# Expert activation in two column halves, transposes copied by two engines, gate products first for 128 slots

## The chip, the cores and the metric

The kernel runs on one core of a Trainium2 chip. The metric is the device time of one execution in microseconds (us). The core's engines work side by side, each on its own queue in order: TensorE (PE; its weight loads are listed as PEld), VectorE (DVE), ScalarE (ACT), GpSimd (POOL) and SyncE (SP), which here issues DMAs. Semaphores order them against each other. Matmul results land in PSUM, which has eight banks of 512 float32 columns on 128 partitions.

## The reference

One transformer block on 512 tokens of width 1024: a normalised, modulated input, a gated MLP and a gated delta network side by side, and then 32 experts, of which each token uses four. The change touches the experts alone:

```python
def expert_block(args):
    tok, wt, e = args
    xb = h_pad[tok]
    gu = xb @ w_gu[e] + b_gu[e]
    gate = jnp.minimum(gu[:, :D_FF], SWIGLU_LIMIT)
    up = jnp.clip(gu[:, D_FF:], -SWIGLU_LIMIT, SWIGLU_LIMIT)
    act = gate * jax.nn.sigmoid(SWIGLU_ALPHA * gate) * (up + 1)
    return (act @ w_down[e] + b_down[e]) * wt[:, None]
```

The width of gate, up and the output is 1024, the limit 7, alpha 1.702, all in float32.

## The kernel before

The first part (up to about 400 us) computes the block ahead of the experts and the routing. Then `run(p, ...)` is called for 32 experts one after the other. An expert's weights are 12 chunks of 1 MB: eight of gate and up (128 rows of 2048 columns), four of down. They pass through a ring of 14 buffers that SyncE fills in order; a buffer is filled again when the matmuls of its last chunk are done.

Experts are sorted by their number of tokens and each gets a fixed number of slots: 14 get 64, three get 32, seven get 96, four get 128, three get 160 and one 192. 128 slots are a `Wide` unit; the others are `Unit`s of 64 or 32 slots (96 is 64 + 32, 160 is 128 + 32, 192 is 128 + 64). The slots of a `Unit` of n stand on n partitions, and the columns are laid out in 128/n blocks over the partitions, so that its gate and up are tiles of 128 partitions by w = 1024 n/128 columns: 512 columns for 64 slots (gate and up in a bank each), 256 for 32 slots (gate and up in one bank).

`run` issues for each expert, in this order: the gate/up matmuls chunk by chunk (`gu_chunk`, or `gu_parts` for `Wide`, which does all gate columns of a chunk before its up columns); `act` of each unit; `between`, which gives TensorE the transposes of the next expert's rows (line 1306) and, for some, the search of the one after that; `down_start` (a small bias matmul), ahead of `turn` or behind it; `turn`, which transposes the activated tile on TensorE (line 1462; for `Wide` 1528) and copies the transposes from one PSUM bank to SBUF (line 1464; for `Wide` 1530, and 1531 for a residual); then the down matmuls chunk by chunk. A down matmul of chunk f takes one transposed block of 128 columns of the activation as its stationary operand. All engines run in the order of the code (a manual schedule), and a tile layer sets the semaphores.

`act` calls `swiglu`, five operations on one tile: Relu (line 1402) and Sigmoid (1403) on ScalarE give sigmoid(1.702 min(gate, 7)); VectorE clips up (1404), makes the gate product min(gate, 7) times that sigmoid (1405), and the product with up + 1 (1406). `gu` in the profile is a PSUM tile (gate, up, or the transposes), `f` the activation's tiles in SBUF, `at` and `ath` the copied transposes.

Of the kernel before, what the change touches and what calls it, by code (L numbers as in the profile page):

```python
# [11 lines left out]
AF = mybir.ActivationFunctionType  # L12
OP = mybir.AluOpType
# [43 lines left out]
def hybrid_block(tc, x, c, w_ada, b_ada, norm1_w, w_in, gm_vnorm_w, gm_w_spatial, gm_b_spatial,  # L57
# [3 lines left out]
    V, S, G, T = nc.vector, nc.scalar, nc.gpsimd, nc.tensor  # L61
# [236 lines left out]
    for n in range(5):  # L298
        V.tensor_scalar(ta[:, 0, :], ta[:, 2, :], n, 1, op0=OP.logical_shift_right,
                        op1=OP.bitwise_or)  # L300
# [459 lines left out]
    def turn(gs):  # L760
        V.transpose(xd[:, gs, :].rearrange("p c i -> p (c i)"), xtd[:, gs, :].rearrange("p c i -> p (c i)"))

    halves = [slice(0, 8), slice(8, 16)]
    for gs in halves:
        turn(gs)
    fill()
    for n in range(4):
        p1s = []
        for gs in halves:
            p1 = bank([P, 8, 32])  # L770
            p1s.append(p1)
            for c8 in range(8):
                for q in range(4):
                    r = slice(q * 32, q * 32 + 32)
                    mm(p1[r, c8, :], ms[n][r, gs.start + c8, :], xd[r, gs.start + c8, :])
        for gs, p1 in zip(halves, p1s):
            S.activation(w1[:, gs, :], p1, AF.Copy)
        fill()
        p2s = []
        for gs in halves:  # L780
            p2 = bank([P, 8, 32])
            p2s.append(p2)
            for c8 in range(8):
                for q in range(4):
                    r = slice(q * 32, q * 32 + 32)
                    mm(p2[r, c8, :], w1[r, gs.start + c8, :], xtd[r, gs.start + c8, :])
        for gs, p2 in zip(halves, p2s):
            V.tensor_tensor(xtd[:, gs, :], xtd[:, gs, :], p2, op=OP.subtract)
            turn(gs)
        fill()  # L790
# [32 lines left out]
    for g in range(4):  # L823
        gs = slice(g * 4, g * 4 + 4)
        kk = bank([P, 4, 2, CH])
        for c4 in range(4):
            ch, hp = divmod(g * 4 + c4, 2)
            for hb in range(2):
                r = slice(hb * 64, hb * 64 + 64)
# [23 lines left out]
    for g in range(2):  # L853
        for hb in range(2):
            r = slice(hb * 64, hb * 64 + 64)
# [318 lines left out]
    both = range(2)  # L1174
# [62 lines left out]
    act_tiles = [f16[:, 2 + i // 2, (i % 2) * 512:(i % 2) * 512 + 512] for i in range(4)]  # L1237
# [158 lines left out]

        return ((h[0], w[0]), (h[1], w[0]), (h[0], w[1]))

    def swiglu(gate, up, r, u):

        n = gate.shape[0]
        S.activation(r, gate, AF.Relu, scale=-1.0, bias=sevens[0:n, 0:1])  # L1402
        S.activation(r, r, AF.Sigmoid, scale=-1.702, bias=sevens[0:n, 1:2])  # L1403
        V.tensor_scalar(u, up, 7.0, -7.0, op0=OP.min, op1=OP.max)  # L1404
        V.scalar_tensor_tensor(r, gate, 7.0, r, op0=OP.min, op1=OP.mult)  # L1405
        V.scalar_tensor_tensor(u, u, 1.0, r, op0=OP.add, op1=OP.mult)  # L1406
        return u

    class Unit:

# [42 lines left out]
        def act(self):  # L1453
            i = (0, 1) if not self.second else (0, 2) if self.part.first else (2, 3)
            r, u = (act_tiles[j][:, 0:self.w] for j in i)
            self.a = swiglu(self.gate, self.up, r, u)

        def turn(self):
            nj = self.w // P
            t = psG.tile([P, 4, P], F32, name="gu")[:, 0:nj]  # L1460
            for j in range(nj):
                T.transpose(t[:, j, :], self.a[:, j * P:(j + 1) * P], ident)  # L1462
            self.at = mp.tile([P, 4, P], F32, name="at", tag="hx" if self.second else "ath", bufs=1)[:, 0:nj]
            S.activation(self.at, t, AF.Copy)  # L1464

        def down_mm(self, l, src, start, stop):
            n, w = self.n, self.w
# [29 lines left out]
    class Wide:  # L1497
# [20 lines left out]
                    mm(self.gu[c * 2 + q], l[:, k, :], r[:, q * 512:q * 512 + 512], False, k == KC - 1 and i == 2)  # L1518

        def act(self):  # L1520
            self.a = [swiglu(self.gu[c], self.gu[2 + c], act_tiles[2 * c], act_tiles[2 * c + 1]) for c in both]

        def turn(self):
            self.at, self.al = (mp.tile([P, KC, P], F32R, name=nm, bufs=1) for nm in ("ath", "atl"))
# [410 lines left out]
```

## Time and profile before

| | us |
|---|---|
| median of three runs | 1533.23 |
| lowest and highest run | 1532.83, 1536.65 |
| the profiled execution | 1535.69 |
| its span, first to last instruction | 1533.9 |
| TensorE busy | 1396.8 (91%) |
| VectorE busy | 698.0 (46%) |
| ScalarE busy | 474.9 (31%) |

Read the busy shares with the stages in mind: the first 400 us are another program than the experts, and a matmul that is listed as busy is not always at its peak. Mean granted TensorE clock: 0.955.

### The profile page before, as it was taken

What the parts mean: (1) busy time and instruction counts of PE and PEld (TensorE: products, weight loads), DVE (VectorE), ACT (ScalarE), POOL (GpSimd) and SP (SyncE); (2) the same over time, 40 slices, a digit from 0 to 9 for tenths busy, and PEclk for the clock granted to TensorE, in tenths of its full rate; (3) what the DMA queues carried; (4) which work ended last, traced back from release to release, by engine and by line L of the source; (5) the groups of instructions that cost most, each with busy time, mean ns of one, the idle gap of its engine ahead of it and who ended that gap; (6) DMA issues with size and microseconds to landing.
All of it is one profiled execution on the core that took longest, in us unless ns stands there. A gap on an engine that the chain in (4) does not pass through costs nothing. (4 is left out here: it accounts for less than half of the span.)

```text
span 1533.9 us, 23341 instructions
## 1 busy us (share of the span) xinstructions
PE 1396.8 (91%) x9113; PEld 729.9 (48%) x9113; DVE 698.0 (46%) x1345; ACT 474.9 (31%) x735; POOL 236.7 (15%) x219
## 2 busy tenths in 40 slices
PE   4898998896899999999999999999999999999982
PEld 3555897674336454337334533642353235424621
DVE  3674639884218454128115612831463136214713
ACT  4343332321116342126014501621351135113501
POOL 2233434340011000110101011000101010101010
PEclk9998999997999999999999999999999999999995
DMA  9566331159699995999999699999988997899972
GB/s 328 181 235 207 98 117 47 52 192 351 245 396 409 401 411 198 400 399 404 390 408 410 253 362 409 407 390 410 398 326 317 403 378 270 314 409 385 382 300 113
DMA packets 113809, 479.54 MB, mean 313 GB/s; under 512 B 15238, under 2 KB 28715, under 8 KB 80922
## 3 DMA queue, kind: packets, MB, share of 16 engines
q1 hardware_dynamic: 98176, 454.10, 75.8%
q0 software_dynamic: 10208, 19.06, 5.0%
q10 hardware_dynamic: 5306, 4.80, 1.0%
q8 instruction: 74, 1.21, 0.3%
q14 instruction: 45, 0.37, 0.1%
HBM read 466.60 MB, written 17.96 MB: 316 GB/s over the span
## 5 line engine op out<-in xcount | busy, mean ns | idle before, releaser
L71 PE MATMUL gu<-ring,h 128*64 128x512 f32 (+1 forms) x1984 | 381.1, 599 | 0.0
L1390 DVE TENSOR_TENSOR wlo<-ring,whi 128x1024 fp32r<-128x1024 f32 x192 | 229.2, 1222 | 49.8 <-ACT whi L1389 48.8
L71 PE MATMUL gu<-ring,at 128*32 128x256 f32 (+1 forms) x1536 | 236.5, 507 | 13.8 <-ACT at L1464 13.8
L1389 ACT ACTIVATE whi<-ring 128x1024 fp32r<-128x1024 f32 x192 | 200.5, 1061 | 113.8 <-PE gu L71 92.0
L71 PEld LDWEIGHTS gu<-ring,h 128*64 128x64 f32 (+1 forms) x1984 | 104.9, 128 | 244.9 <-issue 237.0
L1402 ACT ACTIVATE f<-gu,sevens 128x512 f32<-128x512 f32 (+1 forms) x51 | 32.1, 629 | 533.1 <-PE gu L71 530.9
L1404 DVE TENSOR_SCALAR f<-gu 128x512 f32<-128x512 f32 (+1 forms) x51 | 31.6, 620 | 298.7 <-PE gu L71 281.1
L71 PEld LDWEIGHTS gu<-ring,at 128*32 128x32 f32 (+1 forms) x1536 | 64.2, 125 | 164.8 <-issue 128.6
L1281 POOL DMA_INDIRECT f<-xnd,idx x36 | 36.4, 1012 | 545.3 <-PE gu L1462 280.5
L1750 POOL DMA_INDIRECT acc<-yo,idx x31 | 55.8, 1802 | 401.4 <-DVE yo L1484 237.9
L158 POOL TENSOR_TENSOR wlo<-w,whi 128x1024 fp32r<-128x1024 f32 x32 | 79.3, 2484 | 142.6 <-ACT whi L157 123.1
L71 PE MATMUL gu<-whi,hh 128*128 128x512 f32 x256 | 84.5, 411 | 0.0
L71 PE MATMUL gu<-wlo,hh 128*128 128x512 f32 x256 | 81.1, 398 | 0.8 <-DVE wlo L1390 0.4
L71 PE MATMUL gu<-whi,hl 128*128 128x512 f32 x256 | 80.3, 394 | 0.0
L1484 DVE SCALAR_TENSOR_TENSOR yo<-gu,info,g2x 128x512 f32<-128x512 f32 (+1 forms) x23 | 16.5, 716 | 132.4 <-PE gu L71 132.4
L71 PEld LDWEIGHTS gu<-whi,hh 128*128 128x128 f32 x256 | 45.6, 188 | 33.3 <-ACT whi L1389 18.7
L71 PEld LDWEIGHTS gu<-wlo,hh 128*128 128x128 f32 x256 | 47.6, 188 | 14.2 <-DVE wlo L1390 3.2
L71 PEld LDWEIGHTS gu<-whi,hl 128*128 128x128 f32 x256 | 48.1, 188 | 11.6
L71 PE MATMUL bank<-hhi,whi 128*128 128x512 f32 x160 | 51.5, 442 | 1.8 <-ACT hhi L247 1.8
L71 PE MATMUL gu<-whi,ath 128*128 128x512 f32 x128 | 48.9, 466 | 0.0
L157 ACT ACTIVATE whi<-w 128x1024 fp32r<-128x1024 f32 x32 | 33.7, 1054 | 48.5 <-PE bank L71 26.4
L1462 PE MATMUL gu<-ident,f 128*128 128x128 f32 x114 | 20.1, 301 | 31.4 <-DVE f L1406 31.0
(434 smaller groups left out, 1761.7 us busy)
## 6 DMA issues: line engine op xcount, KB each, us to landing
ring<-in_w_gu_dram SPq DMA_DIRECT2D x256, 1024.0 KB, 16.7
ring<-in_w_down_dram SPq DMA_DIRECT2D x128, 1024.0 KB, 17.8
adaw<-in_w_ada_dram SPq DMA_DIRECT2D x32, 512.0 KB, 4.9
w<-in_w_in_dram SPq DMA_DIRECT2D x24, 512.0 KB, 4.8
ada<-in_w_ada_dram SPq DMA_DIRECT2D x16, 512.0 KB, 10.2
w<-in_w_out_dram SPq DMA_DIRECT2D x8, 512.0 KB, 3.3
x<-in_x_dram SPq DMA_DIRECT2D x4, 512.0 KB, 5.0
x<-in_x_dram ACTq DMA_DIRECT2D x4, 512.0 KB, 4.2
```

The costliest lines, as they stand in the source:

```text
L71: T.matmul(o, l, r, start=start, stop=stop, skip_group_check=True)
L157: S.activation(hi, w, AF.Copy)
L158: G.tensor_tensor(lo, w, hi.bitcast(F32), op=OP.subtract)
L1281: G.indirect_dma_start(out=self.xg, out_offset=None, in_=xnd[:, :], in_offset=bass.IndirectOffsetOnAxis(ap=self.from_[0:self.n], axis=0), ...
L1389: S.activation(hi, w, AF.Copy)
L1390: V.tensor_tensor(lo, w, hi.bitcast(F32), op=OP.subtract)
L1402: S.activation(r, gate, AF.Relu, scale=-1.0, bias=sevens[0:n, 0:1])
L1404: V.tensor_scalar(u, up, 7.0, -7.0, op0=OP.min, op1=OP.max)
L1462: T.transpose(t[:, j, :], self.a[:, j * P:(j + 1) * P], ident)
L1484: V.scalar_tensor_tensor(y, self.dn, self.wt, g2x[self.n], op0=OP.mult, op1=OP.mult)
L1750: G.indirect_dma_start(out=u.rows(acc), out_offset=bass.IndirectOffsetOnAxis(ap=u.idx, axis=0), in_=y, in_offset=None, compute_op=OP.add, ...
```

## The change

`swiglu` is split into four functions, so that its operations can be issued in another order. A `Unit` (32 and 64 slots) now issues the Relu and the Sigmoid for the first half of the columns, then for the second half; on VectorE clip, gate product and product for the first half, then for the second. Its transposes are copied in two halves, the first by ScalarE, the second by VectorE. `Wide` keeps whole tiles of 512 columns, of which it has two: VectorE now does both gate products, then clip and product of the first tile and of the second. The transposes and copies of `Wide` are as before.

```diff
-    def swiglu(gate, up, r, u):
+    def gate_side(gate, r):
 
         n = gate.shape[0]
         S.activation(r, gate, AF.Relu, scale=-1.0, bias=sevens[0:n, 0:1])
         S.activation(r, r, AF.Sigmoid, scale=-1.702, bias=sevens[0:n, 1:2])
+
+    def gate_product(gate, r):
+        V.scalar_tensor_tensor(r, gate, 7.0, r, op0=OP.min, op1=OP.mult)
+
+    def up_side(up, u):
         V.tensor_scalar(u, up, 7.0, -7.0, op0=OP.min, op1=OP.max)
-        V.scalar_tensor_tensor(r, gate, 7.0, r, op0=OP.min, op1=OP.mult)
+
+    def product(r, u):
+
         V.scalar_tensor_tensor(u, u, 1.0, r, op0=OP.add, op1=OP.mult)
-        return u
...
         def act(self):
             i = (0, 1) if not self.second else (0, 2) if self.part.first else (2, 3)
             r, u = (act_tiles[j][:, 0:self.w] for j in i)
-            self.a = swiglu(self.gate, self.up, r, u)
+            self.a = u
+            halves = [slice(0, self.w // 2), slice(self.w // 2, self.w)]
+            for h in halves:
+                gate_side(self.gate[:, h], r[:, h])
+            for h in halves:
+                up_side(self.up[:, h], u[:, h])
+                gate_product(self.gate[:, h], r[:, h])
+                product(r[:, h], u[:, h])
...
-            S.activation(self.at, t, AF.Copy)
+            m = nj // 2
+            S.activation(self.at[:, 0:m], t[:, 0:m], AF.Copy)
+            V.tensor_copy(self.at[:, m:nj], t[:, m:nj])
...
         def act(self):
-            self.a = [swiglu(self.gu[c], self.gu[2 + c], act_tiles[2 * c], act_tiles[2 * c + 1]) for c in both]
+            self.a = [act_tiles[2 * c + 1] for c in both]
+            for c in both:
+                gate_side(self.gu[c], act_tiles[2 * c])
+            for c in both:
+                gate_product(self.gu[c], act_tiles[2 * c])
+            for c in both:
+                up_side(self.gu[2 + c], self.a[c])
+                product(act_tiles[2 * c], self.a[c])
```

In the rows below, which show the built program's order, a name in brackets is the engine whose semaphore is waited for (DMAHW and DMASW are DMA queues).

VectorE's queue in the third expert, which has 64 slots, before (the search's results and indices, then clip, gate product, product; then the next expert's residual):

```order
L1273 COPY info<-t 128x2 [waits PE_49]
L1275 TENSOR_SCALAR idx<-info 64x1 [waits DMASW0_49,DVE_49]
L1425 TENSOR_SCALAR idx<-info,shifts 128x1 [waits DMASW1_49]
L1404 TENSOR_SCALAR f_3753<-gu 128x512 [waits PE_49]
L1405 SCALAR_TENSOR_TENSOR f_3753<-gu,f_3753 128x512 [waits Activation_49]
L1406 SCALAR_TENSOR_TENSOR f_3753<-f_3753 128x512 [waits DVE_49]
L1330 TENSOR_TENSOR hl<-t,hh 128x512 [waits Activation_49]
```

and the same place now:

```order
L1431 TENSOR_SCALAR idx<-info,shifts 128x1 [waits DMASW1_49]
L1409 TENSOR_SCALAR f_3753<-gu 128x256 [waits PE_49]
L1406 SCALAR_TENSOR_TENSOR f_3753<-gu,f_3753 128x256 [waits Activation_49]
L1413 SCALAR_TENSOR_TENSOR f_3753<-f_3753 128x256 [waits DVE_49]
L1409 TENSOR_SCALAR f_3753<-gu 128x256
L1406 SCALAR_TENSOR_TENSOR f_3753<-gu,f_3753 128x256 [waits Activation_49]
L1413 SCALAR_TENSOR_TENSOR f_3753<-f_3753 128x256 [waits DVE_49]
L1479 COPY at<-gu 128x256 [waits Activation_49]
L1330 TENSOR_TENSOR hl<-t,hh 128x512 [waits Activation_49]
```

Three operations have become six of half the width, and VectorE has a copy of the transposes behind them, which waits for ScalarE. The count that the first gate product (1406) waits for is that of the second half's Relu; the count of the copy (1479) is that of ScalarE's copy, whose own count is that of the fourth transpose.

TensorE's queue at the same place, the transposes and the first down matmuls, as a difference:

```order
 L71 MATMUL gu<-b_2219,sel_o 64x512
-L1462 MATMUL gu<-ident,f_3753 128x128 [waits DVE_49]
-L1462 MATMUL gu<-ident,f_3753 128x128 x3
+L1475 MATMUL gu<-ident,f_3753 128x128 [waits DVE_49]
+L1475 MATMUL gu<-ident,f_3753 128x128
+L1475 MATMUL gu<-ident,f_3753 128x128 [waits DVE_49]
+L1475 MATMUL gu<-ident,f_3753 128x128
 L71 MATMUL gu<-ring_3368,at 64x512 [waits DMAHW4_49,Activation_49]
 L71 MATMUL gu<-ring_3368,at 64x512 x3
-L71 MATMUL gu<-ring_3369,at 64x512 [waits DMAHW5_49]
+L71 MATMUL gu<-ring_3369,at 64x512 [waits DMAHW5_49,DVE_49]
```

The transposes now wait twice, once for each half's product; the first down matmul waits for ScalarE's half of the copy, the third chunk's for VectorE's.

VectorE's queue in the fourth expert, with 128 slots, before:

```order
L1390 TENSOR_TENSOR wlo<-ring_3366,whi 128x1024 [waits DMAHW0_49,PE_49,Activation_49]
L1404 TENSOR_SCALAR f_3753<-gu 128x512 [waits PE_49]
L1405 SCALAR_TENSOR_TENSOR f_3753<-gu,f_3753 128x512 [waits Activation_49]
L1406 SCALAR_TENSOR_TENSOR f_3753<-f_3753 128x512 [waits DVE_49]
L1404 TENSOR_SCALAR f_3753<-gu 128x512 [waits PE_49]
L1405 SCALAR_TENSOR_TENSOR f_3753<-gu,f_3753 128x512 [waits Activation_49]
L1406 SCALAR_TENSOR_TENSOR f_3753<-f_3753 128x512 [waits DVE_49]
```

and now:

```order
L1390 TENSOR_TENSOR wlo<-ring_3366,whi 128x1024 [waits DMAHW0_49,PE_49,Activation_49]
L1406 SCALAR_TENSOR_TENSOR f_3753<-gu,f_3753 128x512 [waits Activation_49] x2
L1409 TENSOR_SCALAR f_3753<-gu 128x512 [waits PE_49]
L1413 SCALAR_TENSOR_TENSOR f_3753<-f_3753 128x512 [waits DVE_49]
L1409 TENSOR_SCALAR f_3753<-gu 128x512 [waits PE_49]
L1413 SCALAR_TENSOR_TENSOR f_3753<-f_3753 128x512 [waits DVE_49]
```

Both gate products stand ahead of the first clip, each waiting for its Sigmoid; the first row, the residual of a down chunk, did not move.

## Rows read from the trace of the kernel before

**Rows 1.** Waits: engine, line, releaser, total us, times, longest.

```profile
SPq L1038 <- PE gu L71: 329.9, 173, 11.0
SPq L1041 <- PE gu L71: 219.1, 86, 11.1
...
PEld gu L71 <- DMA ring<-in_w_gu_dram: 8.1, 20, 0.8
```

**Rows 2.** Windows: length, busy us by engine, granted clock, DMA share, GB/s.

```profile
580.00:600.00 20.00, 19.18 (x72) 9.35 (x72) 10.55 (x16) 8.74 (x12) 0.99 (x1) 0.91 0.40 135
714.00:718.00 4.00, 4.00 (x13) 3.11 (x14) 3.15 (x5) 3.43 (x7) 1.01 (x1) 0.57 1.01 420
```

**Rows 3.** Timeline, a 64-slot expert: start, us, engine, line, operation [idle before].

```profile
674.88 0.69 ACT L1402 ACTIVATE f<-gu,sevens 128x512 f32<-128x512 f32 x1 [25.91 <-PE gu L71]
...
675.74 0.69 DVE L1404 TENSOR_SCALAR f<-gu 128x512 f32<-128x512 f32 x1 [10.00 <-PE gu L71]
676.36 0.69 DVE L1405 SCALAR_TENSOR_TENSOR f<-gu,f 128x512 f32<-128x512 f32 x1
677.09 0.69 DVE L1406 SCALAR_TENSOR_TENSOR f<-f 128x512 f32<-128x512 f32 x1
...
677.92 0.63 PE L1462 MATMUL gu<-ident,f 128*128 128x128 f32 x4 [0.87 <-DVE f L1406]
678.59 0.60 ACT L1464 ACTIVATE at<-gu 128x512 f32<-128x512 f32 x1 [2.26 <-PE gu L1462]
...
679.24 1.08 PE L71 MATMUL gu<-ring,at 128*64 128x512 f32 x4 [0.69 <-ACT at L1464]
```

**Rows 4.** Timeline, a 32-slot expert.

```profile
893.17 0.47 ACT L1402 ACTIVATE f<-gu,sevens 128x256 f32<-128x256 f32 x1 [14.97 <-PE gu L71]
893.68 0.42 DVE L1404 TENSOR_SCALAR f<-gu 128x256 f32<-128x256 f32 x1 [5.36 <-ACT f L1402]
893.68 0.51 ACT L1403 ACTIVATE f<-f,sevens 128x256 f32<-128x256 f32 x1
...
894.68 0.42 DVE L1406 SCALAR_TENSOR_TENSOR f<-f 128x256 f32<-128x256 f32 x1
...
895.16 0.44 PE L1462 MATMUL gu<-ident,f 128*128 128x128 f32 x2 [1.02 <-DVE f L1406]
...
895.63 0.38 ACT L1464 ACTIVATE at<-gu 128x256 f32<-128x256 f32 x1 [1.45 <-PE gu L1462]
...
896.07 1.29 PE L71 MATMUL gu<-ring,at 128*32 128x256 f32 x20 [0.47 <-ACT at L1464]
```

**Rows 5.** Groups by form on VectorE: busy us, mean ns | idle before.

```profile
L1327 DVE TENSOR_TENSOR h<-h,sh 128x128 f32<-128x128 f32 x3 | 0.9, 292 | 0.1
```

**Rows 6.** Timeline, a 128-slot expert.

```profile
708.42 0.69 ACT L1402 ACTIVATE f<-gu,sevens 128x512 f32<-128x512 f32 x1 [0.56 <-PE gu L71]
...
709.77 0.67 ACT L1402 ACTIVATE f<-gu,sevens 128x512 f32<-128x512 f32 x1
709.82 0.69 DVE L1404 TENSOR_SCALAR f<-gu 128x512 f32<-128x512 f32 x1 [0.70 <-PE gu L71]
...
710.47 0.72 ACT L1403 ACTIVATE f<-f,sevens 128x512 f32<-128x512 f32 x1
...
711.98 0.63 PE L1528 MATMUL gu<-ident,f 128*128 128x128 f32 x4 [0.56 <-DVE f L1406]
...
713.07 0.69 DVE L1406 SCALAR_TENSOR_TENSOR f<-f 128x512 f32<-128x512 f32 x1
...
713.91 0.63 PE L1528 MATMUL gu<-ident,f 128*128 128x128 f32 x4 [1.30 <-DVE info L1273]
```

**Rows 7.** Timeline, a 96-slot expert: first Relu, transposes of both units, down matmuls.

```profile
642.32 0.69 ACT L1402 ACTIVATE f<-gu,sevens 128x512 f32<-128x512 f32 x1 [24.41 <-PE gu L71]
...
646.23 0.88 PE L1462 MATMUL gu<-ident,f 128*128 128x128 f32 x6
...
647.58 12.70 PE L71 MATMUL gu<-ring,at 128*64 128x512 f32 x96 [0.47 <-ACT at L1464]
```

## The prediction

> **What bounds the kernel now.** I read the waits first. SyncE, which issues the 1 MB weight chunks into the 14 ring buffers, spends 329.9 + 219.1 = 549 us waiting for TensorE's matmuls to give a buffer back, and TensorE's weight loads wait for a gate/up chunk only 8.1 us in 20 short pieces [rows 1]. So the weights are early and TensorE is late: in the stretch after the 192-slot expert the ring is full, the DMA engines are 40% busy, and TensorE is 96% busy (19.18 of 20 us) [rows 2]. I take the expert stage as bound by TensorE's queue: a microsecond that TensorE loses there is a microsecond of the program, since nothing else would be waited for instead. Next I read what stops TensorE in each kind of expert, by its timeline: between the last gate/up matmul and the first down matmul it needs the activation, the transposes and their copy.
>
> **64 slots (14 experts).** Count from the first Relu, 674.88. Clip starts at 0.86, the gate product at 1.48, the product at 2.21, the transposes at 3.04, the copy at 3.71, the first down matmul at 4.36 [rows 3]. TensorE idles 0.87 us before the transposes and 0.69 before the down matmul. The change halves each tile. At 128x256 a Relu takes 0.47, a Sigmoid 0.51, a VectorE operation 0.42, ScalarE's copy 0.38; an operation that needs the one before it starts 0.03 to 0.06 after its end; two transposes take 0.44 [rows 4]. Independent neighbours on VectorE overlap by 0.07 (0.62 apart for 0.69) [rows 3], on ScalarE by about 0.09 (a Relu at 708.42 of 0.69, a Sigmoid of 0.72, the next Relu at 709.77) [rows 6].
>
> What do the halves wait for? Gate is one bank of 512 columns. The first gate product waits for a count that stands after the *second* Relu, not only after the first Sigmoid: both engines read that bank. The copies do the same: ScalarE's copy of two transposes waits for all four, and VectorE's copy waits for ScalarE's, as the order shows. That the tile layer sets such waits between two readers can be seen in the profile: with 32 slots, gate and up share a bank, and the clip, which needs nothing of the Relu, starts 0.03 us after it ends, idle "<-ACT f L1402" [rows 4]. The Trainium skill (PSUM — Partial Sum Buffer, "PSUM bank collisions raise a hardware error") says that two engines on one bank and quadrant collide, reads against reads included, and that the waits go by bank, not by address; the trace of before agrees for 32 slots. It speaks against this change: halves of one bank cannot overlap between engines. By that rule the time is the forecast's; without it, the first rival's.
>
> So: Relu 0 to 0.47, Sigmoid 0.51 to 1.02, second Relu 0.92 to 1.40, second Sigmoid 1.43 to 1.94. VectorE: clip 0.86, gate product 1.43, product 1.89; second clip 2.24, gate product 2.58, product 3.04 to 3.47, where the undivided one ended at 2.90. Six operations of 0.42 are longer than three of 0.69: VectorE becomes the chain. Transposes 3 and 4 start 0.06 [rows 4] to 0.15 [rows 3] later, at 3.53 to 3.62, end at 3.97 to 4.06, ScalarE's half copy ends at 4.39 to 4.48, the first down matmul stands at 4.44 to 4.53. The copy is 0.22 shorter and only half of the transposes stand behind the last product, but that is all used up: 0.08 to 0.17 later than 4.36. I take 0.13, **14 x 0.13 = +1.8 us**. The columns that VectorE copies are needed two chunks later, two matmul pairs of 0.43 after the first, and are ready by 4.9: hidden, and at most 0.4 if not.
>
> **32 slots (3 experts).** Before, the first down matmul stands at 2.90 (896.07 - 893.17) [rows 4]. With 128 columns VectorE takes 0.29 [rows 5]; for ScalarE I take 0.36 (Relu) and 0.40 (Sigmoid), going on from 128x512 to 128x256 [rows 3, 4] by half that step; bounds are a quarter of the full tile and no saving at all, which puts each expert between 0.3 and 0.9. The first clip waits for the second Relu: 1.11. Then by steps of 0.21 (independent) and 0.33 (dependent): 1.32, 1.65, 1.86, 2.07, last product 2.40 to 2.69 instead of 1.93. Last transpose 2.75 to 3.08, copy of 0.27 to 3.39, down at 3.44. **3 x 0.55 = +1.6 us.**
>
> **96 slots (7 experts, a unit of 64 and one of 32).** TensorE has the next expert's transposes and its search to do, so that products are early: transposes of both units begin at 3.91 after the Relu and run without a gap, then 0.47 us idle for the copy, down at 5.26 [rows 7]. After, the 32 unit's last product ends at about 4.97, its last transpose starts at 5.03 and the first down matmul can go at 5.16 instead of 5.26: -0.1 in three of them. In three others the fill is longer (transposes at 4.8) and the shorter copy gives its 0.22 to 0.24. The first expert is ruled by a table load; I give it nothing. **-1.0 us.** If the late product costs more than I think, this becomes 0.
>
> **128 slots (4 experts).** Gate ends first, and ScalarE does Relu, Sigmoid, Relu, Sigmoid until 711.19, in both kernels. Up is ready at 709.82, and VectorE then runs six operations without a gap; the last begins at 713.07, the second transposes at 713.91 [rows 6]. After the change VectorE's queue holds both gate products ahead of the first clip. The second needs the second Sigmoid, 711.19. So VectorE, which cannot pass it, waits from 710.6 to 711.23 with up ready behind it: gate product 711.23, clip 711.84, product 712.57 to 713.26, clip 713.18, product 713.90 to 714.60. The last product ends 0.84 later (before: 713.76), the first by 1.42. What waits is TensorE's transposes, hence ScalarE's copy, the residual and the down matmuls. **4 x 0.84 = +3.4 us.** The other order would gain if both gates were through ScalarE before up is ready; the gap between Relu and clip is 1.40 us and ScalarE needs 2.77.
>
> **160 and 192 slots (4 experts).** The same +0.83 on the second product; behind it on VectorE stand six operations of the second unit instead of three. With 32 slots there, three take 0.35 + 0.46 + 0.42 = 1.23 and six, by the steps above, 1.58. That is +0.35, less some 0.15 because the first half's transpose has run by then: TensorE is **about 1.0 later: 4 x 1.0 = +4.0 us**. The copy of this unit lies beside the wide unit's bias and first down matmuls, so that its halving gains nothing.
>
> **Sum.** 1.8 + 1.6 - 1.0 + 3.4 + 4.0 = **+9.8 us**.
>
> One thing follows such idle time. In 714 to 718, behind a 128-slot activation, the granted clock was 0.57, that is mostly the lower level of 1.2 GHz, after TensorE had stood for 0.56 and 1.30 us [rows 2, 6]. Four microseconds at 0.57 are 1.7 us of matmuls lost. Longer waits can bring such a fall where there is none yet. I add one, **+1.7: +11.5**.
>
> The profiled execution took 1535.69 us (span 1533.9); the runs' median is 2.46 below it. 1535.69 + 11.5 - 2.46 = **1544.7 us**, +0.75%. A measurement of this kernel tells about 0.3% (4.6 us) from no change.
>
> **Rivals.**
> *Faster: the halves overlap.* If the gate product waited only for its own half's Sigmoid and each copy for its own transposes, the 64-slot chain would be: products at 1.20, 1.66, 2.01, 2.35, 2.81 to 3.24, last transposes at 3.30, first half long copied, down at 3.56: -0.8 x 14 = -11.2. 32 slots give -0.45 x 3, 96 slots -0.4 x 7, the wide ones still +7.4: -7.9, that is 1525.3. It decides when the waits are by columns. The order and the 32-slot row speak against it: 6%.
> *No change: TensorE's loss is not the program's.* If the weights were the bound, later matmuls would only use data that lay waiting. 1533. For it: the DMA engines are full in most slices of the page. Against: [rows 1]. With part of the loss hidden or made up by the 96-slot experts: 13%.
> *More: the clock.* If idle time grows behind each of the eight wide experts so that TensorE runs one more stretch at the lower level there, and in two others, 9.8 + 4 x 1.7 = 16.6: 1550. For it: [rows 2]; against: the narrow experts idle hardly longer. 17%.
>
> **Chances and range.** Forecast (1539 to 1548) 64%, clock 17%, no change 13%, faster 6%. Bounds of the small terms: 64 slots 0.08 to 0.25 (+1.1 to +3.5), wide 0.7 to 1.1 each. The range of 1537 to 1551 leaves out the faster rival and most of no change. Slower by over 0.3%: 80%; within: 14%; faster: 6%.
>
> **What would show it.** In the profile after: with 64 slots, the first gate product starts 0.03 after the second Relu; the last product ends 3.4 to 3.5 after the first Relu; ScalarE's copy is 0.38 and starts behind the fourth transpose; down at 4.4 to 4.5. With 128 slots, an idle VectorE ahead of the second gate product, put down to the Sigmoid, and TensorE idle for some 2 us ahead of the first transposes. I am wrong if the down matmuls come at 3.6, or if the waits of weight loads for ring chunks grow.

## The result, and the profile after

The changed kernel took 1545.34 us (median of 6 runs, 1542.22 to 1548.61) against 1533.03 us (6 runs, 1526.71 to 1536.65): 1.0063 of the time before, 95% interval [1.0036, 1.009], that is 5.5 to 13.8 us. (The two medians divided give 1.0080; the ratio on record is the figure used here, and its interval holds both.) The forecast was 1544.7. The profiled execution took 1547.2 us. First its page: span, busy time by engine.

```profile
span 1545.4 us, 23588 instructions
...
PE 1411.3 (91%) x9113; PEld 734.9 (48%) x9113; DVE 719.8 (47%) x1485; ACT 484.7 (31%) x805; POOL 236.9 (15%) x219
```

VectorE has 140 instructions more and ScalarE 70, as the halves need; TensorE has as many matmuls as before, yet is busy 14.5 us longer. The waits after, which answer to [rows 1]:

```profile
SPq L1038 <- PE gu L71: 345.9, 178, 12.1
SPq L1041 <- PE gu L71: 233.1, 89, 12.6
...
PEld gu L71 <- DMA ring<-in_w_gu_dram: 13.2, 26, 0.8
```

SyncE waits 30 us longer for TensorE (579 instead of 549): TensorE is still the late one. The weight loads' waits for chunks grew, though, from 8.1 to 13.2 us. The prediction had named that as a sign against it; the sixth experiment comes back to it.

A 64-slot expert after, the one of [rows 3] (timeline: start, duration, engine, line, operation, idle before it):

```profile
681.39 0.47 ACT L1402 ACTIVATE f<-gu,sevens 128x256 f32<-128x256 f32 x1 [25.74 <-PE gu L71]
...
681.89 0.51 ACT L1403 ACTIVATE f<-f,sevens 128x256 f32<-128x256 f32 x1
...
682.25 0.42 DVE L1409 TENSOR_SCALAR f<-gu 128x256 f32<-128x256 f32 x1 [10.00 <-PE gu L71]
682.31 0.45 ACT L1402 ACTIVATE f<-gu,sevens 128x256 f32<-128x256 f32 x1
...
682.80 0.42 DVE L1406 SCALAR_TENSOR_TENSOR f<-gu,f 128x256 f32<-128x256 f32 x1
...
683.83 0.41 PE L1475 MATMUL gu<-ident,f 128*128 128x128 f32 x2 [0.27 <-DVE f L1413]
...
684.38 0.42 DVE L1413 SCALAR_TENSOR_TENSOR f<-f 128x256 f32<-128x256 f32 x1
...
684.86 0.44 PE L1475 MATMUL gu<-ident,f 128*128 128x128 f32 x2 [0.62 <-DVE f L1413]
685.34 0.38 ACT L1478 ACTIVATE at<-gu 128x256 f32<-128x256 f32 x1 [2.03 <-PE gu L1475]
...
685.75 0.42 DVE L1479 COPY at<-gu 128x256 f32<-128x256 f32 x1 [0.95 <-ACT at L1478]
...
685.77 0.65 PE L71 MATMUL gu<-ring,at 128*64 128x512 f32 x2 [0.47 <-ACT at L1478]
```

The first gate product starts at 682.80, 0.04 us after the *second* Relu ends (682.31 + 0.45), though its own Sigmoid had ended at 682.40 (681.89 + 0.51). The last product ends 3.41 us after the first Relu, ScalarE's copy waits for the fourth transpose, VectorE's copy for ScalarE's, and the first down matmul comes at 4.38 (before: 4.36). TensorE's idle 0.87 + 0.69 has become 0.27 + 0.62 + 0.47.

A 32-slot expert, against [rows 4]:

```profile
900.43 0.37 ACT L1402 ACTIVATE f<-gu,sevens 128x128 f32<-128x128 f32 x1 [14.97 <-PE gu L71]
...
901.14 0.35 ACT L1402 ACTIVATE f<-gu,sevens 128x128 f32<-128x128 f32 x1
...
901.52 0.29 DVE L1409 TENSOR_SCALAR f<-gu 128x128 f32<-128x128 f32 x1 [5.95 <-ACT f L1402]
...
902.77 0.29 DVE L1413 SCALAR_TENSOR_TENSOR f<-f 128x128 f32<-128x128 f32 x1
...
903.81 1.06 PE L71 MATMUL gu<-ring,at 128*32 128x256 f32 x15 [0.37 <-ACT at L1478]
```

Gate and up share a bank here, so that even the first clip stands behind the second Relu (1.09 after the first began). Down comes at 3.38 instead of 2.90.

A 128-slot expert, against [rows 6]:

```profile
714.97 0.69 ACT L1402 ACTIVATE f<-gu,sevens 128x512 f32<-128x512 f32 x1 [0.56 <-PE gu L71]
...
717.78 0.69 DVE L1406 SCALAR_TENSOR_TENSOR f<-gu,f 128x512 f32<-128x512 f32 x1 [0.64 <-ACT f L1403]
718.38 0.68 DVE L1409 TENSOR_SCALAR f<-gu 128x512 f32<-128x512 f32 x1
...
719.94 0.63 PE L1550 MATMUL gu<-ident,f 128*128 128x128 f32 x4 [1.97 <-DVE f L1413]
720.43 0.69 DVE L1413 SCALAR_TENSOR_TENSOR f<-f 128x512 f32<-128x512 f32 x1
...
721.26 1.09 PE L1550 MATMUL gu<-ident,f 128*128 128x128 f32 x4 [0.70 <-DVE info L1273]
...
722.64 0.99 PE L71 MATMUL gu<-whi,ath 128*128 128x512 f32 x1
```

VectorE idles 0.64 us, put down to the Sigmoid, with the clips behind it in its queue. TensorE idles 1.97 us ahead of the first transposes, where it idled 0.56. Then something follows that the sum had only as a lump: the second four transposes take 1.09 us instead of 0.63. The windows of the same place (length; busy us of PE, PEld, DVE, ACT, POOL; granted clock; DMA share; GB/s) say why:

```profile
717.00:721.00 4.00, 1.60 (x16) 1.23 (x14) 3.29 (x6) 1.12 (x2) 0.00 (x0) 1.00 1.02 424
...
721.00:725.00 4.00, 3.74 (x12) 2.97 (x13) 2.66 (x6) 2.81 (x5) 1.02 (x1) 0.57 1.00 416
```

TensorE is busy 1.60 of 4 us, then the granted clock falls to 0.57, mostly the 1.2 GHz level. Before, that stretch lay behind the second transposes [rows 2]; now they and the first down matmuls lie in it. It is like this in three of the four 128-slot experts; the first one keeps a clock of 1.00 and takes 7.01 us to the first down matmul, where this one takes 7.67.

### The profile page after: what moved, and what is told of

Read it like the earlier page. It is cut to its first block, busy times and chain, and to the rows that moved or that the text cites. A ratio compares the mean times of both kernels' runs of the same rounds, so it can differ in the third digit from the quotient of the medians.

```text
span 1545.4 us, 23588 instructions
## 1 busy us (share of the span) xinstructions
PE 1411.3 (91%) x9113; PEld 734.9 (48%) x9113; DVE 719.8 (47%) x1485; ACT 484.7 (31%) x805; POOL 236.9 (15%) x219
## 5 line engine op out<-in xcount | busy, mean ns | idle before, releaser
L1402 ACT ACTIVATE f<-gu,sevens 128x256 f32<-128x256 f32 (+2 forms) x86 | 40.6, 472 | 537.4 <-PE gu L71 528.8
L1409 DVE TENSOR_SCALAR f<-gu 128x256 f32<-128x256 f32 (+2 forms) x86 | 36.8, 428 | 289.0 <-PE gu L71 269.6
L1475 PE MATMUL gu<-ident,f 128*128 128x128 f32 x114 | 27.2, 327 | 32.1 <-DVE f L1413 31.3
L71 PEld LDWEIGHTS gu<-whi,hl 128*128 128x128 f32 x256 | 48.1, 188 | 11.5
```

The costliest lines, as they stand in the source:

```text
L71: T.matmul(o, l, r, start=start, stop=stop, skip_group_check=True)
```

## The experiments

For every kernel I took the same thing from the timelines of all 32 experts: the start of the first down matmul minus the start of the first Relu, here called the stage. Sums over the experts of a kind, minus those before (us; one profiled execution each):

| kernel | 64 (14) | 32 (3) | 96 (7) | 128 (4) | 160, 192 (4) | sum | ratio to before |
|---|---|---|---|---|---|---|---|
| changed | +0.7 | +1.4 | +0.1 | +4.4 | +5.2 | +11.8 | 1.0063 |
| 1 wide order undone | +0.7 | +1.4 | -0.5 | -0.8 | +1.3 | +2.1 | 0.999 |
| 2 wide order only | 0 | 0 | +2.1 | +5.0 | +4.8 | +11.9 | 1.0054 |
| 3 copies only | -3.0 | -0.2 | -0.5 | -0.2 | -0.1 | -4.0 | 0.9938 |
| 4 halves only | +3.7 | +1.7 | +0.4 | -0.6 | +1.1 | +6.2 | 1.0048 |
| 5 gate product by tile | 0 | 0 | +1.0 | +0.1 | +0.7 | +1.9 | 1.0008 |
| 6 idle time filled | +0.7 | +1.5 | +0.2 | +2.4 | +2.2 | +7.0 | 1.0025 |
| 7 copies, two banks | -6.1 | -0.5 | -0.8 | +0.5 | -0.6 | -7.5 | 0.9952 |
| 8 halves, own banks | -11.7 | -0.5 | -0.3 | +0.5 | +1.1 | -10.9 | 0.9915 |

Stages whose code is as before move too, by the clock: in experiment 2 three 96-slot experts take 6.71, 6.74 and 7.07 us at granted clocks of 0.85, 0.83 and 0.79, where before each took 6.15 at 1.00. So a column tells little below 1 or 2 us. And the stage is not the whole expert: the profiled spans differ from the span before by anything from 9.8 us less (experiment 3) to 2.3 us more (experiment 7) than the sums say.

My theory was that of the prediction: the order in `Wide` and the halves on one bank cost, each by its waits, and the copies give a little back. The rivals: that one part has it all, or that the loss comes from something else than these waits, such as more instructions.

**1. The changed kernel with `Wide` in its old order.**

```diff
             for c in both:
                 gate_side(self.gu[c], act_tiles[2 * c])
-            for c in both:
-                gate_product(self.gu[c], act_tiles[2 * c])
-            for c in both:
                 up_side(self.gu[2 + c], self.a[c])
+                gate_product(self.gu[c], act_tiles[2 * c])
                 product(act_tiles[2 * c], self.a[c])
```

> The changed kernel with the order of the wide units (128 slots) put back: clip, gate product, product for the first tile, then for the second. Halves and copies by two engines stay. Theory A (the loss sits in the wide units, where both gate products stand ahead of the first clip): only what the halves cost is left, 0.7 us with 64 slots, 1.4 with 32, 0.2 with 96 and 0.3 in each of the four second units of 160 and 192 slots, +3.5 us on before, about 1536.5 (ratio 1.002). Theory B (the loss comes from halving: more instructions and fixed costs, and the order of the wide units is neutral): as the changed kernel, about 1545 (1.008).

0.999, [0.9969, 1.0012]: no difference from before that this measures, and a little below the 1.002 that I had expected. Halves and copies together cost nothing that shows, so that the wide order is nearly all of the loss of the change as a whole. The -0.8 with 128 slots is the clock: these four stages have the code of before, and the first of them takes 6.19 us where it had 6.86.

**2. The kernel before with only the wide order changed** (both gate products ahead of the first clip).

> The kernel before with one part of the change: both gate products of a wide unit ahead of the first clip. Theory A: 4 x 1.1 to 1.4 us with 128 slots, 4 x 0.85 to 1.0 with 160 and 192, +8.5 us, about 1541.5 (1.0055), and VectorE idle ahead of the second gate product until the second Sigmoid ends. Theory B: 1533 (1.000).

1.0054, [1.0031, 1.0077]. The two runs agree from both sides. VectorE idles 0.64 us ahead of the second gate product, until the second Sigmoid, as expected.

**3. The kernel before with only the copies by two engines:** ScalarE copies the first half of the transposes, VectorE the second, as in the diff of the change.

> The kernel before with one part of the change: the transposes' copy by ScalarE and VectorE, a half each, activation undivided. Theory A: the product ends at 2.90 us as before, ScalarE's copy takes 0.38 for 0.60, VectorE's half is not waited for: -0.22 in each of 14 experts with 64 slots and in six with 96, -0.11 with 32: -4.7 us, about 1528.5 (0.997). Theory B: 52 more instructions on VectorE, each behind ScalarE's copy by the bank's wait, cost what they take: 1533 or more (1.000 or above).

0.9938, [0.9912, 0.9964]: faster, by more than expected. The stage shows the expected step: each 64-slot expert is 0.21 us shorter, since TensorE waits for a copy of 0.38 instead of 0.60 us. VectorE has 35 instructions more (1380 instead of 1345), not the 52 of my expectation. The stages sum to 4.0 us less; the ratio says 9.5 (5.5 to 13.5).

**4. The kernel before with only the activation in halves** (`Unit`; one whole copy).

> The kernel before with one part of the change: activation of 32 and 64 slots in two halves, one whole copy by ScalarE. Theory A: the last product ends 0.5 us later with 64 slots, half of the transposes are done by then, copy 0.60: down matmuls +0.27 x 14 with 64 slots, +0.6 x 3 with 32, +0.3 x 4 in second units, +0.15 x 6 with 96: +7.5 us, about 1540.5 (1.005). Theory B: the whole of the changed kernel's loss, +12 (1.008).

1.0048, [1.0024, 1.0072]. Halves on a bank cost 0.24 us in a 64-slot expert (down at 4.60), copies give back 0.21: together the +0.03 of the changed kernel. Two parts of one edit cancel in this stage.

**5. Is it the gate products' early place, or the wait in front of the clips?** Here each gate product stands ahead of its own clip only, and the rest is as in experiment 2, from which the difference is shown.

```diff
             for c in both:
                 gate_side(self.gu[c], act_tiles[2 * c])
             for c in both:
                 gate_product(self.gu[c], act_tiles[2 * c])
-            for c in both:
                 up_side(self.gu[2 + c], self.a[c])
                 product(act_tiles[2 * c], self.a[c])
```

> The kernel before; in the wide units VectorE does gate product, clip, product of the first tile, then of the second: a gate product ahead of each clip, but the second one no longer ahead of the first clip. Theory A (the loss is the wait of the second gate product for the second Sigmoid, with the first clip queued behind it): gate product at 1.48 after the Relu, clip 2.09, product 2.82, second gate product 3.43, after the second Sigmoid has ended at 2.77, last product ends at 5.46 instead of 5.34: +0.1 in each of eight experts, +0.9 us (1.0005). Rival (a gate product ahead of the clip costs its place by itself, as with both ahead): +8 us (1.005).

1.0008, [0.9985, 1.0031]. The same expert as above in its timeline:

```profile
713.42 0.69 DVE L1406 SCALAR_TENSOR_TENSOR f<-gu,f 128x512 f32<-128x512 f32 x1 [0.78 <-ACT f L1403]
...
714.00 0.72 ACT L1403 ACTIVATE f<-f,sevens 128x512 f32<-128x512 f32 x1
714.03 0.68 DVE L1409 TENSOR_SCALAR f<-gu 128x512 f32<-128x512 f32 x1
...
715.36 0.68 DVE L1406 SCALAR_TENSOR_TENSOR f<-gu,f 128x512 f32<-128x512 f32 x1
```

VectorE works on the first tile while ScalarE does the second Sigmoid (to 714.72), and comes to the second gate product when it is done. The rival's +8 us (1.005) lie outside the interval. So the loss is the second gate product's wait at the head of an in-order queue.

**6. How much of the loss is the clock?** The changed kernel, with twelve transposes of the identity, which nothing uses, where TensorE idles ahead of `Wide`'s first transposes.

```diff
+                for j in range(0 if c else 12):
+                    T.transpose(t[:, j % 4, :], ident, ident)
```

> The changed kernel with 12 more transposes of the identity on TensorE ahead of the first transposes of each wide unit; their results are overwritten. They take about 1.3 us, less than TensorE idles there (1.97 us with 128 slots, 1.0 and then 0.6 with 160 and 192). Theory A: TensorE waits for VectorE's product, so the transposes stand where they stood, and with less idle time the granted clock falls less in and behind the stage: 0 to -5 us against the changed kernel, 1540 to 1545 (ratio on before 1.004 to 1.007). Rival (TensorE's own work sets these stages): +8 x 1.3 us, about 1556 (1.014).

1.0025, [1.0006, 1.0043]: the intervals of this and of the changed kernel just overlap, but with more work on TensorE the time went down, not up, and further than I had expected. The clock is on record for every run: 0.950 to 0.953 in the six of the changed kernel, 0.960 to 0.964 in the twelve of this one. The same expert (first Relu at 712.11), TensorE's timeline and a window:

```profile
714.97 1.51 PE L1550 MATMUL gu<-ident 128*128 128x128 f32 x12
716.99 0.66 PE L1552 MATMUL gu<-ident,f 128*128 128x128 f32 x4 [0.51 <-DVE f L1413]
718.40 0.63 PE L1552 MATMUL gu<-ident,f 128*128 128x128 f32 x4 [0.76 <-DVE info L1273]
...
719.12 0.82 PE L71 MATMUL gu<-whi,ath 128*128 128x512 f32 x2
```

```profile
718.00:722.00 4.00, 3.52 (x17) 2.46 (x17) 3.11 (x7) 3.20 (x6) 1.01 (x1) 1.00 1.02 424
```

The second transposes start 6.29 us after the first Relu, as in the changed kernel, but take 0.63 instead of 1.09, and the clock stays at 1.00 where it was 0.57. Down comes at 7.01 instead of 7.67; before it was 6.32. So of +1.35 here, 0.66 is the clock. Over the eight wide experts: +9.6 in the changed kernel, +4.6 with the fill.

These 4.6 are less than the wait is worth, because the kernel before had lost some time to the clock in these stages too, and the fill takes that away as well. Compare stages that had a clock of 1.00 throughout in both kernels, from the first Relu to the first down matmul. First a 128-slot and the 192-slot expert of the kernel before, then the two with the fill:

```profile
987.83:994.02 6.19, 4.34 (x33) 3.29 (x32) 5.38 (x10) 3.35 (x6) 0.00 (x0) 1.00 1.02 420
572.38:581.25 8.87, 7.34 (x48) 4.21 (x46) 7.23 (x13) 5.97 (x10) 0.40 (x1) 1.00 0.85 335
```

```profile
712.11:719.12 7.01, 5.74 (x46) 4.51 (x44) 5.47 (x10) 3.35 (x6) 0.00 (x0) 1.00 1.01 420
573.20:582.99 9.79, 8.66 (x60) 5.55 (x58) 7.45 (x16) 6.20 (x12) 0.22 (x1) 1.00 0.73 277
```

The wait is worth 0.82 us with 128 slots and 0.92 with 192. With 160 slots, the kernel before had no stage wholly at 1.00; against its shortest, 8.06 at 0.95, the 8.79 of each with the fill leaves at least 0.73. Together that is some 6.4 of the 9.6 us or more for the wait, and some 3.2 or less for the clock.

The weight loads' waits for gate/up chunks, which the prediction had named as a sign, are 7.1 us here, 13.2 in the changed kernel, 12.8 in experiment 2, 9.6 in experiment 1, and 12.8 in experiment 5, which loses nothing and has a mean granted clock of 0.958 in its profile (before: 8.1 at 0.955). So they go neither with the loss nor with a slower clock, and why they differ stays open.

**7. Copies by two engines from two banks:** from the kernel before; the two halves of the transposes go to two tiles of PSUM.

```diff
-            t = psG.tile([P, 4, P], F32, name="gu")[:, 0:nj]
+            m = nj // 2
+            ts = [psG.tile([P, 4, P], F32, name="gu") for _ in both]
...
-                T.transpose(t[:, j, :], self.a[:, j * P:(j + 1) * P], ident)
+                T.transpose(ts[j // m][:, j % m, :], self.a[:, j * P:(j + 1) * P], ident)
...
-            S.activation(self.at, t, AF.Copy)
+            S.activation(self.at[:, 0:m], ts[0][:, 0:m], AF.Copy)
+            V.tensor_copy(self.at[:, m:nj], ts[1][:, 0:m])
```

> The kernel before, activation undivided; the transposes of a 32 or 64 slot unit go to two PSUM banks, a half in each, ScalarE copies one and VectorE the other. Theory A (in one bank ScalarE's half copy waits for all four transposes and VectorE's for ScalarE's): with two banks ScalarE copies while transposes 3 and 4 run, down matmuls come 0.41 us earlier with 64 slots, 0.3 with 32, 0.4 with 96: -9.3 us, about 0.994, 3 to 4 us below the two copies from one bank without the clock. Rival (the wait goes by columns, or the bank does not matter): as the two copies from one bank, 64 slots at 4.14 after the Relu.

0.9952, [0.9933, 0.9971]. The end of a 64-slot stage in it:

```profile
678.64 0.63 PE L1476 MATMUL gu<-ident,f 128*128 128x128 f32 x4 [0.87 <-DVE f L1413]
...
679.09 0.38 ACT L1478 ACTIVATE at<-gu 128x256 f32<-128x256 f32 x1 [2.04 <-PE gu L1476]
679.31 0.42 DVE L1479 COPY at<-gu 128x256 f32<-128x256 f32 x1 [0.81 <-PE gu L1476]
...
679.52 0.65 PE L71 MATMUL gu<-ring,at 128*64 128x512 f32 x2 [0.26 <-ACT at L1478]
```

Now ScalarE starts 0.45 us after the transposes begin, behind two of them, and VectorE's copy waits for TensorE and runs beside it; down comes at 3.92, not 4.35. That part of the expectation held. The time below experiment 3 did not: the medians are level. TensorE's busy time, first of experiment 3, then of this one:

```profile
PE 1391.8 (92%) x9113; PEld 728.6 (48%) x9113; DVE 706.2 (46%) x1380; ACT 468.9 (31%) x735; POOL 237.8 (16%) x219
```

```profile
PE 1399.0 (92%) x9113; PEld 732.2 (48%) x9113; DVE 711.2 (47%) x1380; ACT 469.6 (31%) x735; POOL 237.4 (16%) x219
```

The same 9113 matmuls took 7.2 us less in experiment 3 (mean granted clock 0.961 and 0.956, before 0.955), more than the 3.5 us that its stages are longer. But the profile of experiment 3 is of its fastest run (1522.0) and this one of its slowest (1530.5). Over all runs the clock goes from 0.955 to 0.962 there and from 0.955 to 0.959 here. Whether the two kernels differ at all stays open: the intervals of their ratios overlap.

**8. Halves that do not share a bank:** experiment 7, and for 64 slots each half of the columns has its gate and its up in a bank of its own, so that the second half's Relu reads another bank than the first half's gate product. 32 slots stay whole, `Wide` is as before.

```diff
-                self.gate, self.up = ps[0], ps[1]
...
+            q = 512 // 2
+            self.gate, self.up = [t[:, 0:q] for t in ps], [t[:, q:2 * q] for t in ps]
+            self.both = [t.rearrange("p (i c) -> p i c", i=2) for t in ps]
...
+            for h, o in enumerate(self.both):
...
+                    c = b * w + h * self.q
+                    mm(o[b * n:b * n + n], l, v[:, :, c:c + self.q], start=start, stop=stop)
```

> The kernel before; 64-slot units lay gate and up out so that each half of the columns has its gate and its up in one bank of its own (same matmuls, other columns in each), activation in these two halves; transposes in two banks, copied by two engines; 32-slot units undivided; wide units in the order of before. Theory A (halves pay once no half waits for the other's bank): first gate product at 1.05, last product ends at 3.1 instead of 2.9, but its transposes are two and the first half long copied: first down matmul at 3.4 instead of 4.36 with 64 slots, 2.63 instead of 2.90 with 32, -0.45 with 96: -17 us, ratio 0.989. Rival (halving costs by its instructions, whatever the banks): at or above 1.000, or no lower than the undivided activation with two banks.

0.9915, [0.9889, 0.994]; 1518.73 us, the fastest here, below both kernels. A 64-slot expert in it:

```profile
672.38 0.47 ACT L1402 ACTIVATE f<-gu,sevens 128x256 f32<-128x256 f32 x1 [26.22 <-PE gu L71]
...
672.89 0.51 ACT L1403 ACTIVATE f<-f,sevens 128x256 f32<-128x256 f32 x1
...
673.31 0.45 ACT L1402 ACTIVATE f<-gu,sevens 128x256 f32<-128x256 f32 x1
673.43 0.43 DVE L1406 SCALAR_TENSOR_TENSOR f<-gu,f 128x256 f32<-128x256 f32 x1
...
674.49 0.44 PE L1472 MATMUL gu<-ident,f 128*128 128x128 f32 x2
...
675.02 0.42 DVE L1413 SCALAR_TENSOR_TENSOR f<-f 128x256 f32<-128x256 f32 x1
...
675.93 1.08 PE L71 MATMUL gu<-ring,at 128*64 128x512 f32 x4
```

The gate product now starts at 673.43, 0.03 us after its own Sigmoid, while the second Relu runs (673.31 to 673.76). The first transposes start with no idle time ahead of them, and down comes at 3.55 instead of 4.36, near the 3.56 that the prediction's first rival had for halves that overlap. My expectation for this run was earlier, 3.4, and 2.63 with 32 slots, which took 2.75. That rival was wrong for the change, and right for this layout. The matmuls of this layout write other columns, but TensorE's busy time (1397.7, in experiment 7 1399.0) shows no gain from that. Against experiment 7 the 64-slot stages gain another 5.5 us; the intervals of the two ratios just overlap.

## Why the prediction was right

**TensorE's loss is the program's.** Held in its direction: the stages sum to +11.8 us, the profiled spans differ by 11.5, and SyncE waits longer for buffers. That these two numbers agree so well is luck, as in the experiments they are up to 9.8 us apart. Of the signs of being wrong, the growing waits of weight loads came true, and they turned out to tell nothing: experiment 5 has them without a loss.

**64 slots, +1.8.** The mechanism held step by step, with the gate product behind the second Relu and VectorE as the chain. The size was 0.05 us an expert instead of 0.13, +0.7 in all: the last transposes start 0.06 us after the product, the low end of the step, and the products end at 3.41, at the early end too. Experiments 4 and 8 show that sharing a bank is what takes the gain: halves on one bank cost 3.7 us of these stages, halves with banks of their own gain 5.5 over experiment 7. The waits go by bank, as the Trainium skill (PSUM — Partial Sum Buffer, "PSUM bank collisions raise a hardware error") would have them; that the engines would collide without them was not tried.

**32 slots, +1.6.** Measured +1.4. **96 slots, -1.0.** Measured +0.1. Three of the seven gained 0.08 and two 0.21, as worked out. The first lost 0.37, where I had given nothing, and one lost 0.44 at a granted clock of 0.84, where I had expected it to gain 0.22.

**128 slots, +3.4, and 160 and 192 slots, +4.0.** The queue went as written: gate product at 2.81 us (predicted 2.81), first transposes 1.41 later (1.42), last product ending at 6.15 (6.18), second transposes 0.80 later (0.84). But the stages came out at +4.4 and +5.2. By experiment 6 the wait is worth 0.82 with 128 slots (predicted 0.84), 0.92 with 192 and at least 0.73 with 160 (predicted about 1.0): at least 6.4 of these 9.6, against 7.4 in the sum. The mechanism was right here, and the size nearly so.

**The clock, +1.7.** The term that was least well sized and placed. I added one more stretch at half speed behind a wide stage; it was up to 3.2 us inside the wide stages, since the fall now mostly comes ahead of the second transposes, not behind them. What the clock does behind the first down matmul the stages do not show. The fill took 5.0 us off the wide stages, but at least 1.8 of these the kernel before had lost already.

**The total.** The wide terms were too large by at most 1.0, the clock's too small by at most 1.5, and the small ones too large by 0.1 (2.4 against 2.3): errors that cancel to 0.3 in a sum of 11.5. That the forecast lies within 0.7 us of the median is luck beside that, with an interval of 5.5 to 13.8 us for the difference.

**The rivals.** "The halves overlap" fell by the gate product's start. "No change" fell with the interval above 1. "More: the clock" had the right mechanism for the wide experts, but its 6.8 us were too much: at most 3.2 lie in their stages.

## What to carry to other kernels

Before an operation is moved ahead in an in-order queue, ask what it waits for and who is ready behind it: a VectorE operation that needs the second Sigmoid cost the clips their head start, and with it TensorE 0.82 us in a 128-slot expert at full clock, up to 1.5 where the clock fell as well. Ask of a tile that is split between two engines whether its parts share a PSUM bank: here the activation in halves on one bank cost (1.0048), and with a bank for each half, and copies from two banks, it gained (0.9915). The copy split on one bank still paid (0.9938), since the second half is not needed at once. Try the parts of a change apart: here one part gained 0.6%, and the two others, each by itself, lost 0.5%.

## What was not expected of the hardware

Idle time of TensorE can cost more than its length. In the 128-slot expert shown above it stood for 1.97 and 0.70 us ahead of the two groups of transposes; the clock went from 1.00 to 0.57, and from the start of the second transposes to the first down matmul it took 1.38 us, not 0.72. Twelve matmuls without use in the first gap kept it at 1.00, and the program went from 1.0063 to 1.0025 of the time before, though with intervals that just overlap. The length of the gaps alone does not decide: in the kernel before, two 128-slot experts had the same gaps of 0.56 and 1.30 us, and behind one the clock was 0.57 (714 to 718 us, [rows 2]), behind the other 1.00 (994 to 998 us). In experiment 3 the program gained 9.5 us where its stages sum to 4.0, for which I have no full account.
